# One list of single steps in a new order: the first supertile of a two-layer encoder trunk

## The chip, the cores and the metric

The kernel runs on one NeuronCore of a Trainium2 chip. The core has five engines with a queue of instructions each: PE (TensorE, the matrix engine), DVE (VectorE), ACT (ScalarE), POOL (GpSimd) and SP (SyncE, which here issues nearly all DMAs). Each queue runs in its own order; engines wait for each other on semaphores. The metric is the device time of the program in microseconds (us), as the median of several runs.

## The reference

The program is a trunk of two layers over 2048 tokens of width 1024. A layer normalizes its input, projects it to eight groups of 512 columns, runs two kinds of heads on them, gates and projects back:

```python
hn = rms_norm(x, norm_gain)
aq, ak, av, ag, rq, rk, rv, rg = split(hn @ w_in)          # 8 x 512 columns
ya = chunked_rel_attention(aq, ak, av, rel_bias)           # 8 heads x 64, own chunk of 64 and 8 before it
yr = chunkwise_retention(rq, rk, rv, cos, sin)             # 4 heads x 128, rq and rk turned by rotary tables
x  = x + concat(ya * silu(ag), yr * silu(rg)) @ w_out
```

After both layers there is a last RMS norm. The attention adds a bias per head and distance. The rotary tables are the cosine and sine of position times frequency, here computed in the kernel from the positions.

## The kernel before

Tokens go in 16 tiles of 128, and four tiles make a supertile of 512 (index n, 0 to 3). The heads go in four sweeps (index s). For each layer l, sweep s and supertile n, `dense_T` makes four products with the weights as the fixed operand: j = 0 is the attention's q, j = 1 its k, j = 2 the retention's q, j = 3 its k (results lie transposed, 128 columns by 512 tokens). `dense_V` then makes, for each of the four token tiles a, one product of 512 columns with v, the retention's v and both gates. The attention and retention of that (l, s, n) are run in between the dense products of the next one. In order to keep float32's precision, both operands are split into an upper and a lower float16 half, and each product takes three matmuls per 128 rows of depth: upper by upper, upper by lower, lower by upper. So a section of 512 by 128 takes 24 matmuls.

All engines but SP have their order fixed by the order in which the program issues (a manual schedule); for the first supertile SP does too. Two things set that order:

- In the steady state the generators yield after every eight matmuls. Each yield is a tick (`tick`): functions that were put off with `later(k, fn)` run when their k ticks are over, and `pull` takes steps of the background work in `bg`.
- The first supertile (l, s, n) = (0, 0, 0) has no predecessor to hide its preparation, so its order is written out by hand: a string of names at line 1356, each of which runs one step (`do`, `steps`). It runs before the first tick of `dense_V`.

The names in that string: `xsq`, `xrs`, `xmul`, `xtr`, `xhi`, `xlo` with a tile number are the square sum (ACT), the root (DVE and POOL), the scaled product (DVE, L255), the transposes (PE, L264), the upper half (ACT, L273) and the lower half (DVE, L282) of a token tile. Tiles 4 to 7, of the second supertile, are only squared and scaled in the string; later they take ACT (L270), DVE (L278) and two DMA transposes each on SP (L235, L236). `Wsq`, `Whi`, `Wlo` with j do the same for the weights of section j of `dense_T`, and `Vsq`, `Vhi`, `Vlo` for the four weight blocks of `dense_V`: square sum (ACT, L1234), upper half (ACT, L1314), lower half (DVE, L1317). `lp` and `sc` cast the square sums (DVE, L1238), add them over the partitions with one matmul (PE, L1244) and form the scales (DVE, L1251 to L1255). `d` is the next step of `dense_T`: eight groups of 24 small matmuls (L719; section j by token tile a), then the evacuations of j = 0 and j = 1, then j = 2 and j = 3 in thirds of eight matmuls (L736), each with its evacuation. `t` is the next step of the rotary table of n = 0 (`tables`): DVE steps of 128 x 256 at L93 to L115, sine and cosine on ACT (L117, L118), and at the end eight writes on SP (L125 to L128). `u` is the same for n = 1. `r` turns the relative-bias row around (PE L551 and L557, DVE L552 and L558, SP L560); `bs` and `bt` then build the bias tiles from it. `Tu` and `Vu` form small scale factors; `g` the norm gains.

What follows the string and is touched too: `tab_load` (L620) loads the finished table from DRAM (SP, L623 and L624). Sections j = 2 and 3 are turned by it: a swap of halves by DMA (SP, L673 and L674), `turn` on POOL (L677 to L679), `upper` on ACT (L682), `lower` on DVE (L685), `third` on ACT (L688). For the first supertile the ticks at which these run are the keys of `plan` (L694 to L699).

Of the kernel before, what the change touches and what calls it, by code (L numbers as in the profile page):

```python
# [27 lines left out]
def hybrid_trunk(ctx: ExitStack, tc: tile.TileContext, x, pos, gain, gcol, w_in, w_out, rel, fgain,  # L28
# [569 lines left out]
    def later(k, fn):  # L598
        deferred.append([k, fn])
# [11 lines left out]
    def in_order(apart, terms):  # L611

        return [(kt, w) for w in terms for kt in range(KT)] if apart else [(kt, w) for kt in range(KT) for w in terms]

    def dense_T(l, s, n, g, st):
        hh, hl = hT[l, n]
        nm = f"{l}_{s}_{n}"
        st.tabc = b1.tile([P, 512], F32, tag="tabc", name=f"tabc{nm}")
        st.tabs = b1.tile([P, 512], F32, tag="tabs", name=f"tabs{nm}")
        def tab_load():  # L620
            while n not in tab_done:
                pull(1)
            sp.dma_start(st.tabc, tab_d[n][0])  # L623
            sp.dma_start(st.tabs, tab_d[n][1])  # L624

        first = (l, s, n) == (0, 0, 0)

        def soon(fn):
            if first:
                fn()  # L630
            else:
                later(1, fn)

        def evacuate(j, ps):
            if j == 0:
                st.q = b2.tile([P, 2, 2, 512], F16, tag="q", name=f"q{nm}")
                qq = b1.tile([P, 2, 512], F16, tag="qq", name=f"qq{nm}")
                act.activation(qq[:, 0, :], ps, AF.Copy, scale=2.0 ** -16)

                def q_rest():  # L640
                    dve.scalar_tensor_tensor(out=qq[:, 1, :], in0=ps, scalar=2.0 ** -16, in1=qq[:, 0, :], op0=ALU.mult,
                                             op1=ALU.subtract)
                    for hx in range(2):
                        for half in range(2):
                            sp.dma_start(st.q[half * 64:half * 64 + 64, hx], qq[hx * 64:hx * 64 + 64])

                soon(q_rest)
            elif j == 1:
                st.k = b3.tile([P, 2, 512], F16, tag="k", name=f"k{nm}")
                kk = b1.tile([P, 2, 512], F16, tag="swp", name=f"kk{nm}")  # L650
                kh, kl = kk[:, 0, :], kk[:, 1, :]
                act.activation(kh, ps, AF.Copy, scale=2.0 ** -16)

                def k_rest():
                    dve.scalar_tensor_tensor(out=kl, in0=ps, scalar=2.0 ** -16, in1=kh, op0=ALU.mult, op1=ALU.subtract)
                    sp.dma_start(st.k[0:64, 0, :], kh[0:64, :])
                    sp.dma_start(st.k[64:128, 1, :], kh[64:128, :])
                    sp.dma_start(st.k[64:128, 0, :], kl[0:64, :])
                    sp.dma_start(st.k[0:64, 1, :], kl[64:128, :])

                soon(k_rest)
            else:
                w = 5 - j
                rot = b2.tile([P, w, 512], F16, tag=f"rot{j}", name=f"rot{nm}_{j}")
                if j == 2:
                    raw = rot[:, 1:3].rearrange("p a c -> p (a c)").bitcast(F32)
                else:
                    raw = b1.tile([P, 512], F32, tag="qq", name=f"raw{nm}")
                act.activation(raw, ps, AF.Copy, scale=2.0 ** -16)

                def swap(rot=rot, raw=raw, j=j):
                    swp = b1.tile([P, 512], F32, tag="swp", name=f"swp{nm}_{j}")
                    sp.dma_start(swp[0:64, :], raw[64:128, :])  # L673
                    sp.dma_start(swp[64:128, :], raw[0:64, :])  # L674

                    def turn():
                        pool.tensor_tensor(raw, raw, st.tabc, op=ALU.mult)  # L677
                        pool.tensor_tensor(swp, swp, st.tabs, op=ALU.mult)
                        pool.tensor_tensor(raw, raw, swp, op=ALU.add)  # L679

                    def upper():
                        act.activation(rot[:, 0], raw, AF.Copy)  # L682

                    def lower():
                        dve.tensor_tensor(rot[:, 1], raw, rot[:, 0], op=ALU.subtract)  # L685

                    def third():
                        act.activation(rot[:, 2], rot[:, 0], AF.Copy, scale=2.0 ** -11)  # L688

                    def tokens():  # L690
                        st.kt = b1.tile([P, KT, P], F16, tag="ktok", name=f"kt{nm}")
                        sp.dma_start_transpose(out=st.kt, in_=rot.rearrange("p a c -> p (a c)"))

                    if not first:  # L694
                        plan = {3: turn, 6: upper, 7: lower, **({9: third} if j == 2 else {11: tokens})}
                    elif j == 2:
                        plan = {4: turn, 11: upper, 12: lower, 13: third}
                    else:
                        plan = {3: turn, 5: upper, 6: lower, 7: tokens}  # L699
                    for k_, fn in plan.items():  # L700
                        later(k_, fn)

                if j == 2:
                    st.rq = rot
                    swap()
                    if first:
                        later(1, tab_load)
                else:
                    st.rk = rot
                    later(9 if first else 2, swap)  # L710

        if first:
            ps = [psD.tile([P, 512], F32, tag="dense", name=f"dT{nm}_{j}") for j in range(2)]
            for (j, a) in ((0, 0), (0, 1), (0, 2), (1, 0), (1, 1), (1, 2), (0, 3), (1, 3)):
                cs = slice(a * P, (a + 1) * P)
                m = 0
                for (w_, h_) in ((g.h, hh), (g.h, hl), (g.l, hh)):
                    for kt in range(KT):
                        pe.matmul(ps[j][:, cs], w_[:, j, kt, :], h_[:, kt, cs], start=(m == 0), stop=(m == 23))  # L719
                        m += 1  # L720
                yield
            for j in range(2):
                evacuate(j, ps[j])
                yield
        for j in range(2 if first else 0, 4):
            if j == 2 and not first:
                tab_load()
            if first:
                ps = psR.tile([P, 512], F32, tag="small", name=f"dT{nm}_{j}")
            else:  # L730
                ps = psD.tile([P, 512], F32, tag="dense", name=f"dT{nm}_{j}")
            while g.tdone <= j:
                pull(1)
            m = 0
            for kt, (w_, h_) in in_order(j == 0, ((g.h, hh), (g.l, hh), (g.h, hl))):
                pe.matmul(ps, w_[:, j, kt, :], h_[:, kt, :], start=(m == 0), stop=(m == 23))  # L736
                m += 1
                if m in (8, 16) or (m == 24 and first):
                    yield
            evacuate(j, ps)  # L740
            yield
# [382 lines left out]
    def pull(k):  # L1124
        for _ in range(k):
            while bg:
                try:
                    next(bg[0][0])
                    bg[0][1] -= 1
                    break  # L1130
                except StopIteration:
                    bg.pop(0)
# [7 lines left out]
    def grp(l, s):  # L1140
        if (l, s) not in groups:
            groups[l, s] = Grp()
        return groups[l, s]
# [203 lines left out]
    def do(names):  # L1347
        for nm in names.split():
            steps[nm]()

    def rounds(lists):
# [1 line left out]
            do(names)  # L1353
            yield

    do("xsq0 g g xrs0 g Wsq0 Wlp0 Wsc0 xmul0 xtr0 Whi0 xsq1 xhi0 xrs1 xlo0 xmul1 Wlo0 xsq2 d t Wsq1 xrs2 xtr1 t xhi1 Wlp1 xmul2 "
# [3 lines left out]
    g00.vdone = 4  # L1360
    push(rounds(["xhi4 xrs5 xrs6", "xlo4 xmul5 xrs7", "xdma4 xhi5 xmul6 bt", "xlo5 xhi6", "xdma5 xlo6 xmul7", "xdma6 xhi7",
                 "xlo7", "xdma7 bt", "x8 u", "u x8 bt", "u u x8", "u u x8 bt"]), 12)
# [1 line left out]
    for l in range(DEPTH):  # L1364
        gO = [Grp(), Grp()]
        go = Grp()
        for s in range(NSW):
            g = grp(l, s)
            for n in range(NS):
# [7 lines left out]
                if n == 0 and not first:  # L1377
                    bs, bt = bias_scratch(l, s), bias_tiles(l, s, g)
# [125 lines left out]
```

## Time and profile before

| | |
|---|---|
| median of 3 runs | 2088.74 us (2087.95 to 2091.68) |
| profiled execution, its own time | 2084.99 us |
| profiled execution, span | 2083.2 us |
| PE busy | 2008.0 us, 96% |
| DVE, ACT, POOL busy | 1245.1, 1141.9, 679.1 us |
| clock granted to PE, mean | 0.99 |

The span is the time from the first to the last instruction of one profiled execution. A row of the timeline has the start in us, the length in us, the engine, the line, the operation, output and inputs by the program's names, shapes, and in brackets how long the engine stood idle before it and what ended that. Idle time of an engine matters only where PE, or a chain that PE waits for, is behind it. Matmuls of 512 columns are issued 0.216 us apart, though each is shown 0.38 us long, since they are pipelined. A row of the windows has, for a stretch, the busy time of each engine, PE's granted clock, the share of DMA and GB/s.

### The profile page before, as it was taken

To read this page: it belongs to the slowest core of one execution; us is meant where nothing else is said; L and a number is where in the kernel's file an instruction comes from. 1 tells how busy PE (TensorE), PEld (TensorE's weight loads), DVE (VectorE), ACT (ScalarE), POOL (GpSimd) and SP (SyncE) were. 2 spreads that over 40 slices of the span, in tenths; PEclk is the share of its full clock that TensorE was granted. 3 is DMA by queue.
4 is the path that set the end of the run, shared out by engine and by line. 5 is a ranking of instruction groups with operands and counts; after the bars stand their busy time and mean duration, and the time that the engine had idled before them with its cause. 6 is when DMAs were issued, how large, how long until landed. Compare 5 with 4: busy or idle time off the path is not lost.

```text
span 2083.2 us, 39398 instructions
## 1 busy us (share of the span) xinstructions
PE 2008.0 (96%) x14014; PEld 1051.6 (50%) x14014; DVE 1245.1 (60%) x3817; ACT 1141.9 (55%) x2530; POOL 679.1 (33%) x701
## 2 busy tenths in 40 slices
PE   6988999999999999998999999999999999999998
PEld 4444555555555555544444555555555555554543
DVE  7776666556556655676653656565655566557643
ACT  7556665456565654554444546554655665446432
POOL 0234343444344434330003343434243334333100
PEclk9999999999999999999999999999999999999999
DMA  8768675547575754799774547555655867548974
GB/s 233 166 152 172 143 164 106 117 112 158 114 185 118 158 141 102 158 227 259 200 188 98 124 102 147 119 124 102 142 119 125 182 145 166 122 102 192 213 197 126
DMA packets 645701, 313.63 MB, mean 151 GB/s; under 512 B 459232, under 2 KB 602080, under 8 KB 645504
## 3 DMA queue, kind: packets, MB, share of 16 engines
q1 hardware_dynamic: 645504, 311.12, 66.0%
q8 instruction: 109, 1.79, 0.4%
q14 instruction: 88, 0.72, 0.1%
HBM read 123.26 MB, written 41.98 MB: 79 GB/s over the span
## 4 chain that ended last, share of the span: by engine, by line
PE 48%; DMA 3%; POOL 1%; issue 1%; DVE 1%; ACT 1%; SPq 0%; POOLq 0%; ACTq 0%; DVEq 0%
PE dT L736 14%; PE dV L755 14%; PE dO L1098 13%; DMA pT<-pq 2%; PE r L857 2%; PE S L804 1%; PE S L803 1%; PE o L823 1%; PE o L824 1%; PE o L825 1%; DMA toep<-rel_d 0%; POOL pq L813 0%; PE ptn L999 0%; DMA stO1m<-in_w_out_dram 0%; ACT sc L810 0%
## 5 line engine op out<-in xcount | busy, mean ns | idle before, releaser
L813 POOL TENSOR_TENSOR pq<-sc,pq 128x640 f16<-128x640 f32 (+4 forms) x256 | 319.9, 1250 | 894.6 <-ACT pq L812 479.7
L810 ACT ACTIVATE sc<-sc,mq,cT 128x640 f32<-128x640 f32 (+4 forms) x256 | 218.5, 853 | 623.8 <-DVE rl L829 324.3
L736 PE MATMUL dT<-hTh,whT 128*128 128x512 f16 x1008 | 350.4, 383 | 5.0 <-DMA hTh<-xa 2.2
L755 PE MATMUL dV<-whV,hTh 128*128 128x512 f16 x1024 | 353.1, 381 | 1.7 <-DVE gt L773 1.3
L755 PE MATMUL dV<-wlV,hTh 128*128 128x512 f16 x1024 | 353.0, 380 | 0.0
L755 PE MATMUL dV<-whV,hTl 128*128 128x512 f16 x1024 | 352.8, 380 | 0.0
L736 PE MATMUL dT<-hTl,whT 128*128 128x512 f16 x1008 | 348.4, 381 | 0.0
L736 PE MATMUL dT<-hTh,wlT 128*128 128x512 f16 x1008 | 348.1, 380 | 0.0
L755 PEld LDWEIGHTS <-hTh 128*128 128x128 f16 x2048 | 196.5, 98 | 217.0 <-DVE gt L773 3.8
L736 PEld LDWEIGHTS <-whT 128*128 128x128 f16 x2016 | 193.1, 98 | 217.8 <-issue 12.9
L807 DVE CUSTOM_DVE_ANT_0 sc<-S,bias 128x640 f32<-128x640 f32 (+4 forms) x256 | 188.4, 736 | 125.3 <-PE S L804 124.6
L1098 PE MATMUL dO<-whO,yhy 128*128 128x512 f16 x512 | 194.6, 380 | 1.0 <-DMA yhy<-hTh 0.8
L1098 PE MATMUL dO<-whO,yly 128*128 128x512 f16 x512 | 194.3, 380 | 1.2 <-DMA yly<-hTl 0.6
L1098 PE MATMUL dO<-wlO,yhy 128*128 128x512 f16 x512 | 194.4, 380 | 0.0
L812 ACT ACTIVATE pq<-sc 128x640 f16<-128x640 f32 (+4 forms) x256 | 171.5, 670 | 8.1
L1098 PEld LDWEIGHTS <-yhy 128*128 128x128 f16 x1024 | 99.8, 98 | 116.1 <-DMA yhy<-hTh 1.3
L755 PEld LDWEIGHTS <-hTl 128*128 128x128 f16 x1024 | 99.2, 98 | 110.8 <-issue 1.7
L736 PEld LDWEIGHTS <-wlT 128*128 128x128 f16 x1008 | 97.5, 98 | 112.9 <-issue 6.2
L823 PE MATMUL o<-v,pT 128*128 128x65 f16 x1120 | 130.5, 194 | 15.6 <-DMA pT<-pq 15.5
L803 PE MATMUL S<-k,q 128*128 128x128 f16 (+3 forms) x592 | 143.6, 269 | 0.0
L823 PEld LDWEIGHTS <-pT 128*128 128x128 f16 x1120 | 106.0, 97 | 53.0 <-DMA pT<-pq 24.4
L804 PE MATMUL S<-k,q 128*128 128x128 f16 (+3 forms) x592 | 131.0, 269 | 0.0
(352 smaller groups left out, 3497.3 us busy)
## 6 DMA issues: line engine op xcount, KB each, us to landing
q<-qq SPq DMA_DIRECT2D x128, 128.0 KB, 2.5
yyy<-y_d SPq DMA_DIRECT2D x32, 512.0 KB, 4.9
stT<-in_w_in_dram SPq DMA_DIRECT2D x27, 512.0 KB, 5.0
stV<-in_w_in_dram SPq DMA_DIRECT2D x26, 512.0 KB, 4.5
k<-kk SPq DMA_DIRECT2D x128, 64.0 KB, 2.0
swp<-rot SPq DMA_DIRECT2D x64, 128.0 KB, 2.7
tabc<-tab SPq DMA_DIRECT2D x32, 256.0 KB, 2.7
tabs<-tab SPq DMA_DIRECT2D x32, 256.0 KB, 3.1
```

The source lines that it names most:

```text
L736: pe.matmul(ps, w_[:, j, kt, :], h_[:, kt, :], start=(m == 0), stop=(m == 23))
L755: pe.matmul(ps, h_[:, kt, a * P:(a + 1) * P], w_[:, kt, :], start=(m == 0), stop=(m == 23))
L803: pe.matmul(o, st.q[:, hx, 0, cs], k_, start=True, stop=False)
L804: pe.matmul(o, st.q[:, hx, 1, cs], k_, start=False, stop=True)
L807: dve.tensor_tensor_reduce(out=v, in0=S[:, 0:w], in1=g.bias[hx][:, 640 - w:640], scale=1.0, scalar=-3.0e38, op0=ALU.add, op1=ALU.max, accu ...
L810: act.activation(v, v, AF.Exp, bias=m[:, 0:1], scale=g.c[:, 0:1])
L812: act.activation(pq[:, 0:w], v, AF.Copy)
L813: pool.tensor_tensor(pq[:, w:2 * w], v, pq[:, 0:w], op=ALU.subtract)
L823: pe.matmul(o[:, 0:65], u.p[:, b, :], v_[:, 0:65], start=(b == 0), stop=False)
L824: pe.matmul(o[:, 0:64], u.p[:, b, :], v_[:, 65:129], start=False, stop=False)
L857: pe.matmul(out_, w_, m_, start=(i == 0), stop=(i + 1 == len(pairs)))
L1098: pe.matmul(ps, h_[:, kt, :], w_[:, kt, :], start=(m == 0), stop=(m == 23))
```

## The change

The string of the first supertile is ordered anew, and three numbers that time the turn of its section j = 2 are changed. The same steps run, each once; steps of `t` and `u` that have nothing left to do are no-ops.

```diff
@@ evacuate, in dense_T
                     elif j == 2:
-                        plan = {4: turn, 11: upper, 12: lower, 13: third}
+                        plan = {9: turn, 13: upper, 14: lower, 15: third}
...
                     if first:
-                        later(1, tab_load)
+                        later(2, tab_load)
@@ the list of single steps
-    do("xsq0 g g xrs0 g Wsq0 Wlp0 Wsc0 xmul0 xtr0 Whi0 xsq1 xhi0 xrs1 xlo0 xmul1 Wlo0 xsq2 d t Wsq1 xrs2 xtr1 t xhi1 Wlp1 xmul2 "
-       "Wsc1 xsq3 Wsq2 xrs3 t xtr2 xlo1 xhi2 d Whi1 t xlo2 Wsq3 xmul3 d r Vsq0 Wlp2 Wlo1 t Wsc2 xtr3 Vsq1 r d xhi3 "
-       "t Vlp0 Whi2 Vsc0 t xlo3 Whi3 bs t d Vhi0 Wlo2 d Vhi1 Wlo3 t d d d Vlo0 t t Vsq2 d t Vlo1 t u Vsq3 t d Vlp2 t d t Tu Vsc2 t xsq4 "
-       "Vhi2 Vhi3 d d Vlo2 Vlo3 xsq5 d Vu d xsq6 xrs4 d Vu xmul4 xsq7 d")
+    do("xsq0 g g xrs0 g Wsq0 Wlp0 Wsc0 xmul0 xtr0 Whi0 xsq1 Wlo0 xhi0 xrs1 xmul1 xlo0 xsq2 d xrs2 t Wsq1 xtr1 xmul2 Wlp1 xhi1 "
+       "Wsc1 xtr2 xlo1 xsq3 xhi2 Wsq2 xrs3 d Whi1 xlo2 xmul3 Wlo1 Wsq3 d Wlp2 xtr3 Vsq0 Wsc2 d xhi3 Vsq1 xlo3 Whi2 Vlp0 Whi3 Wlo2 "
+       "Vsc0 d Wlo3 r Vhi0 d Vhi1 r bs d d Vlo0 d Vsq2 d Vlo1 Vsq3 d Vlp2 d t Vsc2 Vhi2 t d Vhi3 Tu t t xsq4 d Vlo2 t Vlo3 t d "
+       "t t xsq5 d Vu t t xsq6 xrs4 d Vu t t xmul4 u xsq7 t t t d t")
```

In the new string the lower half of section 0 (`Wlo0`) stands in front of token tile 0's halves. All but one of the table steps `t` stand behind the sums of the last V sections (`Vlp2`), and the last three behind the last square sums. The reversal of the bias row (`r`) stands behind the upper halves of sections 2 and 3. `Tu` stands behind the last V upper halves (`Vhi2`, `Vhi3`). On SP the eight table writes come behind section 2's swap and the positions of the next table, and the table's load comes one tick later.

## The prediction

> **What bounds the kernel now.** I read the page first: which engine is full, and in which slices it is not.
>
> ```profile
> PE 2008.0 (96%) x14014; PEld 1051.6 (50%) x14014; DVE 1245.1 (60%) x3817; ACT 1141.9 (55%) x2530; POOL 679.1 (33%) x701
> ...
> PE   6988999999999999998999999999999999999998
> ```
>
> The columns of the first row are busy time, share of the span and instructions; the second row is the busy tenths in forty slices of 52 us. The matrix engine (PE) works 2008.0 of 2083.2 us, so the whole kernel is its stream of matmuls, and only its idle 75 us can be won or added to. The change touches the first slices, where the digits are lowest. There I read the timeline of PE, whose brackets say how long the engine stood and for whom.
>
> ```profile
> 25.41 0.54 PE L551 MATMUL rlt<-ident,rl 16*128 16x16 f32 x6
> ...
> 27.40 1.49 PE L557 MATMUL rlr<-anti,rt 128*16 128x128 f32 x12
> 28.82 0.62 PE L719 MATMUL dT<-hTh,whT 128*128 128x128 f16 x8
> ...
> 35.55 0.38 PE L736 MATMUL dT<-hTh,whT 128*128 128x512 f16 x1
> ...
> 41.72 0.16 PE L1244 MATMUL ms<-mbV,ones 128*128 128x2 bf16 x1 [2.54 <-DVE mbV L1238]
> ...
> 43.41 0.63 PE L736 MATMUL dT<-hTl,whT 128*128 128x512 f16 x1
> ...
> 50.33 1.89 PE L755 MATMUL dV<-whV,hTh 128*128 128x512 f16 x8
> ...
> 71.30 1.89 PE L736 MATMUL dT<-hTh,whT 128*128 128x512 f16 x8
> ...
> 83.00 0.38 PE L736 MATMUL dT<-hTh,whT 128*128 128x512 f16 x1 [0.79 <-DVE qq L641]
> ...
> 94.88 0.23 PE L857 MATMUL r<-rv,dT 128*128 128x128 f16 x1 [2.07 <-DVE dT L865]
> ```
>
> The reader is to see a clock for every stage. Section 2 of the first supertile starts at 35.55, the V sections (dV) at 50.33, the second supertile (dT of n = 1) at 71.30. Between the first two lie 48 matmuls. At dV's pace (96 matmuls from 50.33 to 71.30, 0.218 us each) they are worth 10.5 us, and they take 14.8. The difference is the wait of 2.54 us for a cast on VectorE (mbV) and, behind it, matmuls of 0.63 instead of 0.38 us: the clock was at half for a while, some 1.7 us lost. This 4.3 us is what an earlier list can win ahead of dV. The stretch from 20 to 30 us says who feeds PE there:
>
> ```profile
> 20.00:30.00 10.00, 8.06 (x104) 7.08 (x103) 8.85 (x24) 10.00 (x18) 0.66 (x1) 1.00 1.11 325
> ```
>
> The columns are PE, PE's weight load, VectorE (DVE), ScalarE (ACT) and GpSimd (POOL): ACT is full and DVE nearly so. So the order of their steps decides, not PE's.
>
> **The change part by part.** No instruction is added or removed; the first list, three due times and SyncE's (SP's) order move. The prices, from the same timeline for DVE and ACT:
>
> ```profile
> 39.64 1.28 DVE L1317 SCALAR_TENSOR_TENSOR wlV<-hTh,sc2V,whV 128x1024 f16<-128x1024 f32 x1
> ...
> 40.83 0.29 DVE L113 TENSOR_SCALAR wk<-wk 128x256 f32<-128x256 f32 x1
> 41.16 0.43 DVE L115 SCALAR_TENSOR_TENSOR wk<-wk 128x256 f32<-128x256 f32 x1
> 41.50 0.17 DVE L1238 CAST mbV<-m1V 128x2 bf16<-128x2 f32 x1
> ...
> 43.30 0.16 DVE L349 RECIPROCAL ciT<-cT 128x1 f32<-128x1 f32 x1 [1.24 <-ACT cT L195]
> 43.38 0.14 DVE L1247 TENSOR_REDUCE m2sV<-ms 128x1 f32<-128x2 f32 x1
> ...
> 44.18 0.21 DVE L1255 TENSOR_SCALAR sc3V<-sc3V,gi 128x1 f32<-128x1 f32 x1
> ...
> 49.94 0.16 DVE L410 TENSOR_TENSOR gqkV<-gqkV 128x1 f32<-128x1 f32 x1 [1.66 <-ACT reV L407]
> ...
> 50.86 1.28 DVE L255 SCALAR_TENSOR_TENSOR hTh<-hTh,rsn,gb 128x1024 f32<-128x1024 f32 x1
> ```
>
> ```profile
> 41.62 0.51 ACT L118 ACTIVATE wk<-wk,quarter 128x256 f32<-128x256 f32 x1
> ...
> 42.34 0.19 ACT L193 ACTIVATE qkT<-sc3W 128x1 f32<-128x1 f32 x1
> ...
> 43.41 1.04 ACT L248 ACTIVATE hTh<-hTh 128x1024 f16<-128x1024 f32 x1
> ...
> 44.45 2.17 ACT L1314 ACTIVATE whV<-hTl,sc2V 128x1024 f16<-128x1024 f32 x2
> ...
> 56.00 1.28 ACT L764 ACT_TABLE_LOAD   x1
> ```
>
> *First section.* Behind the first lower half, the list leaves out the rounding step, then three table steps and the reversal of the bias row (the 16-row matmuls at 25.41 and 27.40) until later. I walked each queue in its new order with each step's own duration and its inputs' times. The lower half of section 1 is done at 24.5, so its first group starts at 24.6 instead of 28.82: 4.2 us sooner. It does not last. The scale of V0 needs V1's squares, which now stand behind the upper half of token 3 on the full ACT and end at 27.4; PE waits there some 1.6 us. Then the 16-row matmuls come in: the second lot needs a copy that DVE reaches only behind two lower halves (31.6), so PE waits 1.1 us and spends 0.54 + 1.49 us. Section 2 starts at 36.2, against 35.55: 0.6 us later.
>
> *Section 2 to dV.* mbV no longer stands behind eight table steps and comes at 38.9 instead of 41.50. PE asks for it after 16 matmuls, at 36.2 + 3.5 = 39.7: the 2.54 us are gone, and with them the half clock. Sections 2 and 3 end at 36.2 + 10.5 = 46.7. dV needs the V upper halves: ACT runs the last two for 2.17 us from 40.7, as soon as the scales are there (44.18 less 43.38, 0.8 us behind the sum), to 42.8; the last lower half is done at 47.3 and is wanted at 50. So dV starts at 46.7 instead of 50.33: **3.6 us won**.
>
> *The tables.* They now run behind this. DVE: scales until 40.9; its reciprocal waits for c on ACT, which stands behind the two upper halves and their small copies (1.07 us from 42.34 to 43.41), until 43.6; two table steps at 0.43 to 44.5; lower half 1.20, step, lower half 1.20 to 47.3; rounding and four steps, 0.6 + 1.7, to 49.6; a norm step and the V units (50.86 less 49.94) 1.1 to 50.7; step and clamp to 51.4; token 4's product, issued in front of the last table step, 1.2 to 52.7; the last step to 53.1. ACT, busy with the squares of tokens 4 to 7 until 52.3, takes the cosine (0.51) at 53.2 instead of 41.62. Behind it stand the table's last copy, section 3's evacuation and token 4's upper half, then dV's first evacuation: dV's table load comes at about 55.7, much as before (56.00). But PE is 3.6 us ahead now. dV has two PSUM buffers, and its third group wants the first one back at 46.7 + 10.4 = 57.1. DVE's rests read it after that evacuation, behind token 4's lower half and token 5's product:
>
> ```profile
> 58.06 0.29 DVE L769 SCALAR_TENSOR_TENSOR v<-dV,v 128x128 f16<-128x128 f32 x1 [1.58 <-ACT rv L765]
> ...
> 80.85 0.69 DVE L685 TENSOR_TENSOR rot<-raw,rot 128x512 f16<-128x512 f32 x1 [1.64 <-POOL pq L813]
> ```
>
> They end near 58.9, as before 58.06 + 0.8. PE waits 1.8 us; the third and fourth groups, with 0.3 us for the next buffer, end at 69.6. Half of the gain is left there: 71.30 less 69.6.
>
> *SP's queue.* Every table step that moved takes its DMAs with it: eight writes of the table and two loads stand in front of the eight transposes of tokens 4 to 7, of their bias load and of section 3's swap. Section 2's swap now stands in front of the table writes; that is early and hidden.
>
> ```profile
> 44.08 0.54 SPq L125 DMA_DIRECT2D tab<-wk  x1
> ...
> 51.11 0.38 SPq L624 DMA_DIRECT2D tabs<-tab  x1
> 53.86 1.35 SPq L235 DMA_TRANSPOSE hTh<-hTh  x1
> ...
> 67.45 1.28 SPq L235 DMA_TRANSPOSE hTh<-hTl  x1
> ...
> 70.20 0.54 SPq L673 DMA_DIRECT2D swp<-raw  x1
> ```
>
> ```profile
> bias<-toep SPq DMA_DIRECT2D x2, 320.0 KB, 4.7
> ...
> tab<-wk SPq DMA_DIRECT2D x8, 64.0 KB, 2.1
> ...
> hTh<-hTl SPq DMA_TRANSPOSE x2, 3.3
> ```
>
> (The last number of the DMA rows is us from issue to landing.) Table writes used to start at 44.08 and SP was free for transposes at 51.5, before the first was ready (53.86). Now they start when the cosine is done, 53.7. Eleven issues took 7.03 us, 0.64 each, so the eighth goes out at 58.2 and lands 2.1 later, at 60.3; the table's second load, which reads it, leaves SP free at 60.7. What was hidden by 2.4 us of slack is now in the open: token 4's upper half has been ready since 55.4. The transposes go out back to back at 1.37 us (two from 67.45 to 70.20). In front of token 7's upper half stand six of them and the bias load (0.6): issue at 69.5 instead of 67.45, landing 3.3 later, 72.8. The second supertile's first matmuls read it. They start at **72.8 instead of 71.30: 1.5 us later**, after a wait of 3.2 us.
>
> *The turns.* The table's turn of section 2 is five ticks later by its new due time. GpSimd first clears the bias tile, now landing near 68.2 (4.6 behind its issue at 63.5), then does both turns in a row.
>
> ```profile
> 73.66 1.27 POOL L677 TENSOR_TENSOR raw<-raw,tabc 128x512 f32<-128x512 f32 x1 [11.40 <-DMA swp<-raw]
> ...
> 77.74 0.18 POOL L582 MEMSET bias<- 64x64 f32 x1
> ```
>
> ```profile
> 78.16 0.83 ACT L584 ACTIVATE bias<-bias,ciT 128x640 f32<-128x640 f32 x1 [5.42 <-POOL bias L583]
> ```
>
> Section 3's swap is issued behind the transposes at 72.3 instead of 70.20. POOL started 3.5 us behind that issue, so 75.8; turn and clear take 4.1, as from 73.66 to 77.74; ACT's bias scale, which waits for the clear, goes from 78.16 to 80.3. Behind it on ACT stand now both upper halves and the first softmax. DVE does section 2's lower half and two table steps at 81.6 to 83.1, then section 3's lower half at 83.1 instead of 80.85: **2.2 us late**. The next q evacuation reuses that buffer, and PE's third group of n = 1 waits for it already (0.79 at 83.00). So PE goes on at 85.2, and DVE, ACT and SP carry the same 2.2 us.
>
> PE itself may be later: 3.2 us of idle time can bring the half clock, 1.7 us, as behind 41.72. It would then come 1.5 + 1.7 = 3.2 us late to the place where it used to wait 0.79, and leave it 2.4 us late. Its next wait, 2.07 us at 94.88 for DVE's dT, which comes 2.2 late, takes up the difference. The Trainium skill (TensorE: Matmul & The Clock Gate, "HAM oscillation") has the clock fall only behind idle gaps over about 3.4 us. By it a wait of 3.2 us would stay free, the forecast would stand, and the second rival below would lose its ground. The trace does not agree, since 43.41 shows the fall behind a wait of 2.54 us; the measurement decides.
>
> **Sum.** -3.6 (dV's start) +1.9 (dV's two buffers: 22.9 us from 46.7 to 69.6 against 20.97) +3.2 (transposes behind the table) +0.7 (turns) = +2.2 us. From there on the orders are the same, and I carry this through. The profiled execution took 2084.99 us, so 2087.2 there; it lies 3.75 under the median of the runs, 2088.74, and on that median the forecast is **2090.9 us**. The unknown price is how bursts on SP land: an upper half landed 3.3 behind its issue; I take that, since it is the same operation on the same tiles. Below, dV's end bounds it: n = 1 cannot start before 69.6, so at most 3.2 us less. Above, seven transposes that each hold the queue half as long again (0.7 us) would be 5 us more.
>
> **The rivals.**
> *The head start is kept* (faster). The place is SP at 53.7. If the table's last step runs some 4 us sooner than my walk (by 49.6), SP is free at 56.7, the transposes land by 68.8, and PE starts n = 1 at dV's end. Without the two-buffer wait too, that is 46.7 + 20.9 = 67.6: -3.7 us, and with the 0.79 and part of the 2.07 us behind it also gone, about -5: 2083.7. Against it: token 4's product and the V units stand in front of the last table steps, and each is as long as it was.
> *PE's lag is not absorbed* (slower by more). If the half clock (1.7 us) falls on n = 1 and DVE's dT waits in turn for PE's late products, the 2.2 grow by 1.7, and a second half clock behind a longer wait at 94.88 adds as much: 2.2 + 1.7 + 1.7 = +5.6, 2094.3. It decides if that wait grows from 2.07 past 2.54. Against it: the masked product that dT reads is issued at the end of section 1, well ahead.
> *Nothing lasts.* The 3.5 us from the swap's issue to POOL's start were counted in a crowd of transposes. If that takes 2 us less, the bias scale is where it was, since ACT stood 5.42 us for it, DVE is in time, and the 1.5 us of PE go into its waits of 0.79 and 2.07: 2088.7.
>
> **How the numbers follow.** Between runs of the kernel before there are 3.7 us, so about 0.2% (4.2 us) is what can be told from no change. Chances: forecast 0.46 (its own range 2088.7 to 2093.5; a sixth of it, 0.08, above +4.2 us), nothing lasts 0.11, lag not absorbed 0.30 (all slower), head start kept 0.13 (all faster). So faster 0.13, within 0.2% 0.49, slower 0.38. The range takes in the rivals' times and the runs' spread of 3 us above the median on the slow side: 2083.7 to 2097.
>
> **What would show it.** Right: dV at 46.7 and no wait at mbV; a wait of about 2 us at dV's third group; cosine near 53; table writes on SP from 53.7 and transposes back to back from 60.7; PE waiting 3 us for hTh at 72.8; bias scale on ACT at 80. Wrong: transposes issued before 58, or PE's first idle row of n = 1 missing; then the head start is kept. If the wait at 94.88 is over 2.5 us and slow matmuls follow, the second rival holds.

## The result, and the profile after

The changed kernel is slower by 4 to 5 us: its median is 2092.39 us where the kernel before, run beside it, has 2088.34 (4.05 us apart), and the ratio of the two, which goes by all executions, is 1.0024 (5.0 us) with a 95% interval of 1.0014 to 1.0034. A second comparison gave 1.0020 (1.0004 to 1.0036); one of the twelve executions of the changed kernel there took 6671.25 us and counts as a slow run, which the ratio leaves out. The forecast was +2.2 us, so the sign and the range hold and the size is about half of what was measured. But it gave a chance of 0.38 only to slower by more than 0.2%, and 0.49 to a change within 0.2%.

PE's work is the same; the idle time grew. This is the page's first line and PE's timeline, as it was read for the kernel before. The first row of the timeline is PE's first sum of weights; it waits for the first weights from DRAM, and these land at another time in every profile (9.41 us before, 10.67 here). **So I compare times counted from that row**; on PE's clock the changed kernel's profile lies 1.26 us later for no reason of its own.

```profile
PE 2008.9 (96%) x14014; PEld 1051.8 (50%) x14014; DVE 1245.2 (59%) x3817; ACT 1141.9 (54%) x2530; POOL 678.3 (32%) x701
```

```profile
10.67 0.16 PE L1244 MATMUL ms<-mbW,ones 128*128 128x1 bf16 x1 [3.43 <-DVE mbW L1238]
...
38.63 0.38 PE L736 MATMUL dT<-hTh,whT 128*128 128x512 f16 x1
...
42.08 0.17 PE L1244 MATMUL ms<-mbV,ones 128*128 128x2 bf16 x1
...
49.01 1.89 PE L755 MATMUL dV<-whV,hTh 128*128 128x512 f16 x8
...
61.29 0.39 PE L755 MATMUL dV<-whV,hTh 128*128 128x512 f16 x1 [1.75 <-DVE gt L773]
...
66.82 0.39 PE L755 MATMUL dV<-whV,hTh 128*128 128x512 f16 x1 [0.18 <-DVE gt L773]
...
76.60 3.57 PE L736 MATMUL dT<-hTh,whT 128*128 128x512 f16 x8 [4.43 <-DVE xa L93]
...
100.94 0.23 PE L857 MATMUL r<-rv,dT 128*128 128x128 f16 x1 [1.47 <-DVE dT L865]
```

The reader sees all the stations of the forecast. The wait of 2.54 us for mbV is gone and dV starts 2.6 us sooner (49.01 less 1.26 against 50.33). Then 1.75 and 0.18 us are lost at dV's two buffers, and at n = 1 PE stands 4.43 us and starts 4.0 us late (76.60 less 1.26 against 71.30). The name in the last bracket but one, a table step of VectorE, is only what ended at the same time; SP's queue shows what PE waited for:

```profile
56.10 0.49 SPq L125 DMA_DIRECT2D tab<-wk  x1
...
62.97 0.33 SPq L624 DMA_DIRECT2D tabs<-tab  x1
63.34 1.35 SPq L235 DMA_TRANSPOSE hTh<-hTh  x1
...
68.09 1.68 SPq L236 DMA_TRANSPOSE hTl<-hTh  x1
69.81 1.34 SPq L235 DMA_TRANSPOSE hTh<-hTl  x1
71.69 1.24 SPq L236 DMA_TRANSPOSE hTl<-hTl  x1
73.05 1.27 SPq L235 DMA_TRANSPOSE hTh<-hTl  x1
74.42 1.28 SPq L236 DMA_TRANSPOSE hTl<-hTl  x1
75.80 0.54 SPq L673 DMA_DIRECT2D swp<-raw  x1
```

The table's writes start at 56.10, the table's load is issued at 62.97, and the first transpose directly behind it. Token 7's upper half is issued at 73.05, and PE starts 3.55 us later. Section 3's swap is at 75.80, against 70.20 before: 4.3 us late. From there the lag goes through POOL, ACT and DVE, in these three timelines. POOL's row is the clear of the bias tile; it stood 0.75 us for the tile's load, which SP issues behind the swap:

```profile
83.56 0.15 POOL L582 MEMSET bias<- 64x64 f32 x1 [0.75 <-DMA bias<-toep]
```

```profile
55.57 0.51 ACT L118 ACTIVATE wk<-wk,quarter 128x256 f32<-128x256 f32 x1 [0.97 <-DVE wk L115]
...
83.94 0.83 ACT L584 ACTIVATE bias<-bias,ciT 128x640 f32<-128x640 f32 x1 [10.05 <-POOL bias L583]
```

```profile
86.91 0.68 DVE L685 TENSOR_TENSOR rot<-raw,rot 128x512 f16<-128x512 f32 x1
```

VectorE's lower half of section 3 (the row of DVE) comes at 86.91 less 1.26 instead of 80.85: 4.8 us late. PE's wait at 100.94 is as late, 4.8 us. From there the orders are the same, and 4.8 us is the size of the result. This lower half is the landmark of all that follows. The two profiled executions end further apart than that: counted from the first sum of weights 11.6 us (spans of 2096.1 and 2083.2 us). But the second profile of the changed kernel, with nearly the same landmark (+4.73), ends only 2.3 us behind before (span 2085.5, first sum at 9.43). So what comes behind the landmark varies by several us from one execution to the next, and a single profile's end says little.

### The profile page after: what moved, and what is told of

It reads as the page before. It is cut to its first block, busy times and chain, and to the rows that moved or that the text cites. A ratio compares the mean times of both kernels' runs of the same rounds, so it can differ in the third digit from the quotient of the medians.

```text
span 2096.1 us, 39397 instructions
## 1 busy us (share of the span) xinstructions
PE 2008.9 (96%) x14014; PEld 1051.8 (50%) x14014; DVE 1245.2 (59%) x3817; ACT 1141.9 (54%) x2530; POOL 678.3 (32%) x701
## 4 chain that ended last, share of the span: by engine, by line
PE 48%; DMA 3%; DVE 1%; ACT 1%; issue 1%; SPq 0%; POOL 0%; POOLq 0%; ACTq 0%; DVEq 0%
PE dT L736 15%; PE dV L755 14%; PE dO L1098 13%; PE r L857 2%; DMA pT<-pq 2%; PE S L804 1%; PE S L803 1%; PE o L823 1%; PE o L824 1%; PE o L825 1%; DMA toep<-rel_d 1%; PE ptn L999 0%; DMA stO1m<-in_w_out_dram 0%; POOL pq L813 0%; DMA yly<-hTl 0%
## 5 line engine op out<-in xcount | busy, mean ns | idle before, releaser
L736 PE MATMUL dT<-hTh,whT 128*128 128x512 f16 x1008 | 351.8, 385 | 8.9 <-DVE xa L93 4.4
L736 PE MATMUL dT<-hTh,wlT 128*128 128x512 f16 x1008 | 348.1, 381 | 0.0
L736 PE MATMUL dT<-hTl,whT 128*128 128x512 f16 x1008 | 347.7, 380 | 0.0
L736 PEld LDWEIGHTS <-whT 128*128 128x128 f16 x2016 | 193.1, 98 | 223.0 <-issue 13.8
L736 PEld LDWEIGHTS <-wlT 128*128 128x128 f16 x1008 | 97.8, 98 | 109.2 <-issue 2.5
```

## The experiments

My theory: the table, late on SP's queue, holds up the transposes of tokens 4 to 7, and through them the swap, the bias tile and VectorE. Two rivals: the new order of the first section costs it, or the three due times do. The table shows each kernel's stations in us from the first sum of weights, one profile each; the ratio is to the kernel before in the same comparison, with its 95% interval.

| kernel | section 2 | dV | n = 1 | lower half | less before | ratio |
|---|---|---|---|---|---|---|
| before | 26.14 | 40.92 | 61.89 | 71.44 | 0 | 1 |
| changed | 27.96 | 38.34 | 65.93 | 76.24 | +4.80 | 1.0024 (1.0014 to 1.0034) |
| changed, again | 27.99 | 38.37 | 65.56 | 76.17 | +4.73 | 1.0020 (1.0004 to 1.0036) |
| table late alone | 26.75 | 37.14 | 64.26 | 75.42 | +3.98 | 1.0009 (0.9997 to 1.0022) |
| changed, table early | 28.53 | 39.26 | 59.98 | 69.38 | -2.06 | 0.9990 (0.9980 to 1.0000) |
| changed, due times of before | 27.82 | 38.20 | 65.41 | 75.75 | +4.31 | 1.0023 (1.0009 to 1.0036) |
| before, due times alone | 27.19 | 40.28 | 61.00 | 69.94 | -1.50 | 1.0002 (0.9989 to 1.0015) |
| changed, writes twice | 27.93 | 38.32 | 70.52 | 80.88 | +9.44 | 1.0055 (1.0035 to 1.0076) |
| before, writes twice | 27.18 | 40.27 | 61.67 | 71.61 | +0.17 | 0.9998 (0.9985 to 1.0011) |
| V sums sooner | 27.19 | 37.63 | 61.98 | 70.59 | -0.85 | 0.9997 (0.9984 to 1.0009) |
| V sums sooner, new due times | 26.14 | 36.58 | 57.83 | 67.47 | -3.97 | 0.9990 (0.9978 to 1.0002) |
| the same, again | 26.14 | 36.57 | 57.83 | 68.02 | -3.42 | 0.9990 (0.9976 to 1.0004) |
| the same, and Wlo0 sooner | 24.55 | 34.99 | 56.24 | 66.34 | -5.10 | 0.9980 (0.9965 to 0.9995) |

In every row the landmark lies within the interval of the ratio, so the times agree with a loss that is made before 90 us and carried through. A microsecond between single profiles tells nothing: the first section in the order of before put section 2 at 26.14 in three profiles and at about 27.19 in three others.

**The table alone.** The list of before, with its table steps moved to where the change has them, and the new due times (the end of the string is the changed list's, so `Vhi2`, `Vhi3` and `Tu` have their places there, too):

```diff
-    ... xsq2 d t Wsq1 xrs2 xtr1 t xhi1 ... Wlo3 t d d d Vlo0 t t Vsq2 d t Vlo1 t u Vsq3 t d Vlp2 t d t Tu Vsc2 t xsq4 ...
+    ... xsq2 d t Wsq1 xrs2 xtr1 xhi1 ... Wlo3 d d d Vlo0 Vsq2 d Vlo1 u Vsq3 d Vlp2 d t Vsc2 Vhi2 t d Vhi3 Tu t t xsq4 d Vlo2 t Vlo3 t d
+    t t xsq5 d Vu t t xsq6 xrs4 d Vu t t xmul4 xsq7 t t t d t
```

> The list of before; only its table steps stand where the changed list has them (behind the V sections' upper halves), with the three new due times. First theory (the table on SP's queue sets the second supertile's start): cosine on ACT near 54 to 56 us, table writes on SP from there, transposes back to back from about 62 to 63, PE waits 3 us or more for token 7's upper half and starts n = 1 at 74 to 76 us; the whole about 2 to 5 us slower than before. Rival (the first section's order loses the time, the late table costs nothing): n = 1 starts at 71 to 72 and the time is within 1 us of before.

Its PE timeline shows the same picture with the first section untouched:

```profile
47.02 1.89 PE L755 MATMUL dV<-whV,hTh 128*128 128x512 f16 x8
...
59.30 0.39 PE L755 MATMUL dV<-whV,hTh 128*128 128x512 f16 x1 [1.76 <-DVE gt L773]
...
74.14 2.48 PE L736 MATMUL dT<-hTh,whT 128*128 128x512 f16 x8 [3.96 <-DVE xa L93]
```

dV is 3.8 us sooner than before, and still n = 1 is 2.4 and the lower half 4.0 us late. That is the theory's number. The time, 0.0009 or 1.9 us over before, has an interval from nothing to 4.6 us, so it agrees with the landmark but would not carry the verdict alone.

**The table put back.** The changed list with its `t` steps between the V sections again, and some in the first section, which the shown lines leave out:

```diff
-    ... Vsc0 d Wlo3 r Vhi0 d Vhi1 r bs d d Vlo0 d Vsq2 d Vlo1 Vsq3 d Vlp2 d t Vsc2 Vhi2 t d Vhi3 Tu t t xsq4 ...
+    ... Vsc0 t d Wlo3 r t Vhi0 d Vhi1 r t bs d d Vlo0 t t d Vsq2 t d Vlo1 t Vsq3 t d Vlp2 t d t Vsc2 Vhi2 t d Vhi3 Tu xsq4 ...
```

> The changed list with its table steps put back between the V sections, as early as the list of before has them; the three new due times stay. First theory (late table on SP's queue): cosine near 42 to 44, no wait of over 1 us of PE for token 7's upper half, n = 1 at 71 to 73 us, and the time 3 to 6 us under the changed kernel, within 2 us of before. The casts for the V sums then stand behind table steps again, so a wait of 1 to 2.5 us at mbV may come back. Rival (first section's order and due times): still 3 to 5 us slower than before, with n = 1 early and the loss showing up behind 80 us.

```profile
45.24 0.48 SPq L125 DMA_DIRECT2D tab<-wk  x1
...
54.59 1.35 SPq L235 DMA_TRANSPOSE hTh<-hTh  x1
...
64.96 1.28 SPq L235 DMA_TRANSPOSE hTh<-hTl  x1
```

Token 7's upper half is issued 7.2 us sooner than in the changed kernel (55.20 against 62.38 from the first sum), n = 1 starts at dV's end without a wait, and the lower half falls from +4.8 to -2.1. The ratio falls from 1.0024 to 0.9990. The feared wait at mbV came back with 0.18 us only. So the table's place makes the loss; without it the rest of the change is none, and perhaps a gain of some 2 us (the interval, 0.9980 to 1.0000, just reaches 1).

**The due times.** Once the changed list with the old ones, once the list of before with the new ones:

```diff
-                        plan = {9: turn, 13: upper, 14: lower, 15: third}
+                        plan = {4: turn, 11: upper, 12: lower, 13: third}
...
-                        later(2, tab_load)
+                        later(1, tab_load)
```

> The changed list whole, only the three due times (the turn of section 2, the lower and upper halves, the third section's turn and the table's load) as before. First theory: the late table is unchanged, so n = 1 starts at 75 to 77 us behind a wait of 4 us and the time is within 1 us of the changed kernel, or slower by up to 2 us because the turns stand in GpSimd's queue ahead of the table. Rival (the due times cost it: the turn five ticks later makes the bias scale and the lower half of section 3 late): bias scale on ACT back at about 80, VectorE's lower half at 83, and the time 2 us or more under the changed kernel.

> The kernel before with the three new due times alone, its list as it was. First theory (the due times cost nothing): products beside the turn take 1.2 to 1.3 instead of 1.86 to 2.29 us, but dV's groups did not wait for them; n = 1 starts at 71 and the time is within 1.5 us of before. Rival (the due times bring part of the loss, by a later turn and bias scale): VectorE's lower half of section 3 comes 1 to 2 us later than 80.85 and the time is 1 to 2 us over before.

With the old due times the changed list is as slow as with the new ones (1.0023 against 1.0024), so that rival is out. PE's row at n = 1 in this run names the landing of the upper half of token 6 or 7 as what ended the wait, where the changed kernel's row named a table step:

```profile
75.02 1.89 PE L736 MATMUL dT<-hTh,whT 128*128 128x512 f16 x8 [3.06 <-DMA hTh<-hTl]
```

On the list of before the new ones shortened the products of tokens 5 and 6, as expected, and moved the landmark 1.5 us the other way than the rival had it; the time does not show that (1.0002, from 0.9989 to 1.0015).

**Twice the load on SP.** The most direct test of the queue is a dose. The eight writes of the first table are issued twice, in the changed kernel and in the one before:

```diff
         for hf in range(2):
             sl = slice(hf * 64, hf * 64 + 64)
             cs = slice(hf * 256, hf * 256 + 256)
-            sp.dma_start(tab_d[n][0, 0:64, cs], k2[sl, :])
+            for _ in range(2 if n == 0 else 1):
+                sp.dma_start(tab_d[n][0, 0:64, cs], k2[sl, :])
...
```

> The changed kernel, with the eight table writes of the first table issued twice (the same data; eight issues more on SP, at 0.64 us each 5.1 us, in front of the transposes of tokens 4 to 7). First theory (SP's queue is the path to the second supertile): first transpose about 5 us later than in the changed kernel, the wait of PE at n = 1 grows from 4.4 to about 9 us, n = 1 starts near 81 us, and the time is 4 to 6 us over the changed kernel, so some 8 to 11 us over before. Rival (the late chain on ScalarE and VectorE sets it, SP only looks full): under 1 us over the changed kernel.

> The kernel before, with the same eight extra writes. First theory (there SP has slack: it stood free from 51.5 to 53.86 and again between the transposes): the first transpose moves from 53.86 to 56.6 at most, the gaps before the later ones take that up, token 7's upper half is issued within 0.5 us of 67.45, n = 1 starts at dV's end and the time is within 1 us of before. Rival (5 us on SP always show): 3 to 5 us over before.

SP (the first transpose, then token 7's upper half) and PE (the start of n = 1) of the changed kernel with the dose, then the first transpose and token 7's upper half of the kernel before with it. The added line moves the later line numbers up by one, so L236 and L737 here are L235 and L736 elsewhere:

```profile
67.39 1.35 SPq L236 DMA_TRANSPOSE hTh<-hTh  x1
...
76.59 1.29 SPq L236 DMA_TRANSPOSE hTh<-hTl  x1
```

```profile
80.12 3.57 PE L737 MATMUL dT<-hTh,whT 128*128 128x512 f16 x8 [9.05 <-DVE gt L774]
```

```profile
58.35 1.36 SPq L236 DMA_TRANSPOSE hTh<-hTh  x1
...
67.41 1.29 SPq L236 DMA_TRANSPOSE hTh<-hTl  x1
```

The same eight issues delay the first transpose in both, by 5.4 us (57.79 against 52.44 from the first sum, changed kernel again) and by 4.6 us, which is 1.9 us more than was expected of the kernel before. In the changed kernel nothing takes that up: the wait at n = 1 grows to 9.05 us, the landmark goes from +4.7 to +9.4 and the time from about 5 to about 11 us over before (1.0055, with only six executions; their median is 9 us over). In the kernel before, the gaps between the transposes take up all of it: token 7's upper half is issued at 58.11 from the first sum instead of 58.04. So before the change SP had at least 4.6 us of slack between the table and token 7's upper half, and the change uses up all of it and more. The queue is shown as the path, and not merely as a full queue.

**A version with the table early and the V sums soon.** The wait at mbV can go without moving the table: in the list of before, V2's sum (`Vlp2`) and scale and the last upper halves stand some steps sooner.

```diff
-    ... Vlo0 t t Vsq2 d t Vlo1 t u Vsq3 t d Vlp2 t d t Tu Vsc2 t xsq4 Vhi2 Vhi3 d d Vlo2 Vlo3 xsq5 ...
+    ... Vlo0 t Vsq2 d Vsq3 Vlp2 t d t u d Vsc2 Vlo1 t t Vhi2 Vhi3 t t d Tu t xsq4 d Vlo2 Vlo3 xsq5 ...
```

> The list and due times of before; only the sum and scale of V2 and the upper halves of V2 and V3 stand some steps sooner, ahead of the last table steps. First theory: the wait of 2.54 us for mbV shrinks to under 1 us and the half clock behind it goes, dV starts at 47 to 48.5 us instead of 50.33, while cosine and table writes stay within 1.5 us of 41.62 and 44.08, so the transposes still follow their inputs and n = 1 starts at 69.5 to 71; the time is 0 to 3 us under before. Rival (dV's two buffers or the transposes give all of it back): dV starts 2 us sooner, but n = 1 starts at 71 to 72 and the time is within 1 us of before.

The rival was right: dV starts 3.3 us sooner and n = 1 where it was. PE stood at dV's fourth group, and VectorE and POOL show why:

```profile
65.86 0.39 PE L755 MATMUL dV<-whV,hTh 128*128 128x512 f16 x1 [3.27 <-DVE gt L773]
```

```profile
57.09 2.31 DVE L255 SCALAR_TENSOR_TENSOR hTl<-hTl,rsn,gb 128x1024 f32<-128x1024 f32 x1
59.33 2.29 DVE L278 TENSOR_TENSOR hTh<-hTh,hTh 128x1024 f16<-128x1024 f32 x1
61.54 2.28 DVE L278 TENSOR_TENSOR hTl<-hTl,hTl 128x1024 f16<-128x1024 f32 x1
63.74 1.27 DVE L255 SCALAR_TENSOR_TENSOR hTl<-hTl,rsn,gb 128x1024 f32<-128x1024 f32 x1
```

```profile
57.05 1.27 POOL L677 TENSOR_TENSOR rot<-rot,tabc 128x512 f32<-128x512 f32 x1
58.28 2.25 POOL L678 TENSOR_TENSOR swp<-swp,tabs 128x512 f32<-128x512 f32 x1
60.61 2.13 POOL L679 TENSOR_TENSOR rot<-rot,swp 128x512 f32<-128x512 f32 x1
```

Three steps of VectorE take 2.3 us while POOL turns section 2, and the fourth, behind the turn, 1.27. The dV rests stand behind them. The Trainium skill (SBUF — State Buffer, "SBUF: two separate sides") says that GpSimd and a VectorE step with two inputs from SBUF share one pair of ports: whichever starts first has it for its whole instruction, and the other waits. The rows agree: the two engines' steps end in turn, POOL at 58.32, VectorE at 59.40, POOL at 60.53, VectorE at 61.62, POOL at 62.74, VectorE at 63.82, each about 1.1 us behind the other, so that steps of 1.2 to 1.3 us take up to 2.3. The new due times put the turn five ticks later, so here they should pay:

> The list with the sum of V2 and the upper halves moved sooner (the table early), now with the three new due times. In the run with the old due times VectorE's products of tokens 5 and 6 took 2.3 us instead of 1.28 and 1.23 while GpSimd turned section 2 beside them, and PE stood 3.27 us at dV's fourth group. First theory (the turn beside the products stretches them; five ticks later it runs behind them): the products between 57 and 63 us take 1.2 to 1.3 us, the wait at dV's fourth group falls under 1.5 us, n = 1 starts 1.5 to 3 us sooner than with the old due times (68 to 69.5), and the time is 2 to 4 us under before. Rival (the later turn makes the bias scale late, and that sets the rest): n = 1 sooner, but VectorE's lower half of section 3 stays where it was at 79.7 and the time is within 1 us of before.

VectorE's timeline with them, then POOL's:

```profile
58.26 1.27 DVE L255 SCALAR_TENSOR_TENSOR hTl<-hTl,rsn,gb 128x1024 f32<-128x1024 f32 x1
59.45 1.21 DVE L278 TENSOR_TENSOR hTh<-hTh,hTh 128x1024 f16<-128x1024 f32 x1
60.65 1.22 DVE L278 TENSOR_TENSOR hTl<-hTl,hTl 128x1024 f16<-128x1024 f32 x1
...
64.20 2.32 DVE L278 TENSOR_TENSOR hTl<-hTl,hTl 128x1024 f16<-128x1024 f32 x1 [0.34 <-ACT hTl L270]
```

```profile
62.37 1.84 POOL L677 TENSOR_TENSOR rot<-rot,tabc 128x512 f32<-128x512 f32 x1
64.16 1.27 POOL L678 TENSOR_TENSOR swp<-swp,tabs 128x512 f32<-128x512 f32 x1
```

The steps ahead of the turn are short again and the one beside it is long. PE's wait at the fourth group falls to 0.17 us, n = 1 starts 4.1 us sooner and the landmark is at -4.0. The time is 0.9990 of before, with an interval that just takes in 1. It was repeated beside the changed kernel:

> The kernel with the V sums sooner and the three new due times, once more, beside the changed kernel on one chip. First theory: as in its first run, 2 to 4 us under before and 7 to 9 us under the changed kernel. Rival (its 0.1% was chance): the same as before within 1 us.

> The changed kernel once more, on one chip with the others. First theory: 4 to 6 us over before, with the wait of over 4 us at n = 1 and token 7's upper half issued 4 us later after the weights' first sum. The slow matmuls behind the wait need not be the same. Rival (part of its loss was chance): 1.5 to 3 us over before, as the run with the late table steps alone.

The changed kernel repeated its loss: the wait at n = 1 is 4.04 us, token 7's upper half is issued at 62.08 from the first sum against 58.04 before, and the ratio is 1.0020. The other kernel has 0.9990 again (0.9976 to 1.0004). By the medians it is 5.8 us under the changed kernel, less than the 7 to 9 that stood, and 0.4 us under before; so its landmark gain shows in both profiles, but a gain in time over before is not shown.

**The lower half alone.** Last, the part of the change that stands in front of all this: only `Wlo0` is put ahead of token 0's upper half, in that version; the bias row stays where before has it.

```diff
-    do("xsq0 g g xrs0 g Wsq0 Wlp0 Wsc0 xmul0 xtr0 Whi0 xsq1 xhi0 xrs1 xlo0 xmul1 Wlo0 xsq2 ...
+    do("xsq0 g g xrs0 g Wsq0 Wlp0 Wsc0 xmul0 xtr0 Whi0 xsq1 Wlo0 xhi0 xrs1 xlo0 xmul1 xsq2 ...
```

> The list with the V sums sooner, the table early and the new due times; of the changed kernel's first section only the sooner lower half is added (Wlo0 ahead of token 0's upper half), the bias row stays where before has it. First theory (the sooner lower half is harmless, what cost the changed kernel's first section was the bias row behind the V scales): PE's wait of 1.74 us for the lower half's scale goes, a wait of about 0.5 us for token 0's lower half comes, section 2 starts 0 to 1.2 us sooner after the weights' first sum than without it, dV likewise, and the time is 0 to 1.5 us under that kernel. Rival (VectorE is full there and the sooner lower half only pushes the tokens): section 2 starts at the same place or up to 1.2 us later, and the time is 0 to 1.5 us over it.

Section 2 starts at 24.55, 1.6 us sooner than in either profile without it, and all of it arrives: dV, n = 1 and the landmark are 1.1 to 1.7 us sooner. At 0.9980 (0.9965 to 0.9995) this is faster than the kernel before, by about 4 us (2.8 by the medians), and about 8 us faster than the changed kernel beside it (medians of 2081.71 and 2089.93 us). The first theory was right in kind: the wait of 1.74 us is gone, the one of 0.5 us did not come, and the gain is a little more than it allowed. The changed kernel has the same sooner lower half and starts section 2 at 27.96; the rows of its first section that this version lacks are the waits for V0's scale and for the bias row:

```profile
30.12 0.16 PE L1244 MATMUL ms<-mbV,ones 128*128 128x2 bf16 x1 [1.55 <-DVE mbV L1238]
...
34.53 1.47 PE L557 MATMUL rlr<-anti,rt 128*16 128x128 f32 x12 [0.97 <-DVE rt L552]
```

By these rows they make 2.5 of the 3.4 us between the two; no run moves the bias row alone. What makes the rest stays open.

## Why the prediction was right or wrong

Times here are the changed kernel's less 1.26 us.

The mechanism of the forecast is the one that the runs showed: a head start at dV, the table behind it on SP, and a second supertile that waits for the transposes. Its size was half, as two terms were too small: section 1's first group, and the burst on SP with its landing.

*First section (+0.6, measured +1.8): right in kind, small in size.* The waits were 1.55 and 0.97 where 1.6 and 1.1 stood. But section 2 started at 37.4 and not at 36.2. Section 1's first group is the step that failed: it was put at 24.6, when its lower half is ready. PE's timeline has it here:

```profile
18.74 1.87 PE L264 MATMUL ptn<-ident,xa 128*128 128x128 f32 x8
...
25.73 1.07 PE L264 MATMUL ptn<-ident,xb 128*128 128x128 f32 x8 [0.46 <-DVE xb L255]
...
27.08 0.61 PE L719 MATMUL dT<-hTh,whT 128*128 128x128 f16 x8
```

The group is at 27.08, or 25.8, behind the transposes of token 3 (25.73), which stand in front of it in PE's queue and for which PE waits; the walk named only the lower half. The matmuls in front of that were slower, too: the eight transposes at 18.74 took 1.87 us where the profile of before has 1.04. In all five profiles with the changed order, the one with its table early among them, they take 1.75 to 1.92 us; in the order of before they take 1.04 in some profiles and 1.92 in others (with the due times alone, for one). What that costs in the changed order is not shown.

*Section 2 to dV (-3.6): right.* No wait at mbV, no half clock; section 2 to dV took 10.4 us where 10.5 stood. dV came at 47.75 instead of 46.7 only because it began 1.2 late.

*dV's two buffers (+1.9): right*, 1.75 and 0.18 us.

*SP's queue (+3.2): right in kind; the largest mis-sized term.* Cosine, writes and first transpose were 1.1, 1.1 and 1.4 us later than forecast, which is mostly the late section again (the cast of mbV, at 40.2 where 38.9 stood, was already 1.3 late). Then the seven issues in front of token 7's upper half took 9.7 us (63.34 to 73.05) where 8.8 stood: in the burst the queue went from 68.09 to 69.81 and from 69.81 to 71.69 for one transpose each, 1.7 and 1.9 us and not 1.37. The landing took 3.55 and not 3.3. So n = 1 started at 75.3 instead of 72.8, and the wait was 4.43 and not 3.2.

*The turns (+0.7): right in kind.* Swap, bias scale and lower half were 74.5, 82.7 and 85.7 where 72.3, 80.3 and 83.1 stood: 2.2 to 2.6 more, of which SP has the 2.2 already at the swap. Behind it the turn was not what the clear of the bias tile waited for, as the forecast had it, but the tile's load (0.75 us). The 2.2 us carried through became 4.8. The due times, which this step made responsible for a part, cost nothing that the runs show.

*The half clock at n = 1* came (3.57 us for eight matmuls), and it was absorbed as said. With the due times of before PE started n = 1 at full speed, and the landmark was late by 4.31 all the same.

*The rivals.* Keeping the head start needed the table's last step some 4 us sooner than the walk; it came later. "Lag not absorbed" gave 5.6 us, which is near the measured size, but its mechanism did not happen: the wait that it watches was 1.47 us and not over 2.54. "Nothing lasts" is out with the swap 4.3 us late.

## What to carry to other kernels

Moving a step in a list moves its DMAs, and a queue that had slack can become the path: find the first transfer behind the moved ones that PE waits for, and count the queue's gaps up to it. Extra copies of a cheap transfer measure that slack directly; here the same eight cost nothing in one kernel and about 5 us at the landmark of the other. And when an early start is lost in a later wait, look for what stretched there: the landmark came 3 to 4 us sooner when the V sums were sooner, the table stayed early, and the turn was out of VectorE's way, and 0.85 us sooner with the turn in it.

## What the runs showed of the hardware that was not expected

The length of PE's wait does not tell whether its clock falls. Behind 4.43 us in the changed kernel it fell, and eight matmuls took 3.57 us instead of 1.89; behind 3.06 us with the old due times it stayed full. But behind 2.54 us in the kernel before it fell, and with the old due times a wait of 1.76 us, at the start of n = 2, was followed by eight matmuls in 3.59 us.

What tells is how long PE worked in a fixed stretch of 3.41 us. In all thirteen profiles the granted clock changes only at whole multiples of 3.41 us from its other changes, and it is half for one, two or three such stretches. These are windows cut on that grid, of the kernel before, then of the changed list with the old due times; the columns behind the window are its length, the busy times of PE, its weight load, VectorE, ScalarE and GpSimd, the granted clock, the DMA share and GB/s.

```profile
39.66:43.07 3.41, 1.35 (x8) 0.64 (x8) 2.33 (x7) 1.81 (x7) 0.00 (x0) 1.00 0.96 285
43.07:46.48 3.41, 3.41 (x10) 1.22 (x9) 1.82 (x8) 3.38 (x6) 0.00 (x0) 0.50 0.42 108
```

```profile
70.32:73.73 3.41, 1.64 (x8) 0.55 (x6) 2.31 (x8) 3.28 (x11) 0.00 (x0) 1.00 0.93 171
73.73:77.14 3.41, 2.12 (x12) 1.08 (x13) 2.06 (x6) 0.00 (x0) 0.00 (x0) 1.00 0.98 198
...
135.18:138.59 3.41, 1.58 (x13) 0.72 (x11) 3.30 (x11) 0.81 (x4) 0.55 (x1) 1.00 1.07 231
138.59:142.01 3.42, 2.63 (x7) 0.98 (x8) 1.36 (x5) 2.27 (x7) 1.16 (x1) 0.50 0.96 191
```

Before, most of the wait of 2.54 us fell into one stretch, PE was busy for 1.35 of its 3.41 us (40%), and the next stretch was granted half the clock. The wait of 3.06 us was shared between two stretches with 48% and 62%, and the clock stayed. The wait of 1.76 us began in a stretch that held shorter ones, too (0.70 and 0.17 us): PE was busy for 46% of it, and the clock fell. From 30 us on, over all thirteen profiles, the clock fell behind each stretch in which PE was busy for less than 40% and behind none above 48%; in between both occur.

The grid lies differently to the program in each profile, so the same order can bring the half clock at a place in one execution and not in another: of the changed kernel's two profiles, one has it at 901 us and the other does not, and the other has it at 625 us. The matmuls of the first section, too, reach full speed at a moment that differs between profiles of the same order: where section 2 stands at 26.14 the second eight transposes took 1.04 to 1.05 us, where it stands at 27.19 they took 1.91 to 1.92.
